# A hybrid decoder layer: gate 21 behind the last pair, values by both token halves, a third early group

## The chip, the cores and the metric

The kernel runs on one core of a Trainium2 chip. The metric is the device time of one execution in microseconds (us). A core's engines work from queues of their own: TensorE (PE) multiplies matrices, VectorE (DVE) and GpSimd (POOL) do elementwise work, ScalarE (ACT) activations and copies, and SyncE (SP) issues the transfers between HBM and the on-chip memory (SBUF). PE writes into banks of PSUM, from which DVE and ACT read.

## The reference

The layer works on 1024 tokens of 1024 features, float32:

```python
h = h + hybrid_mixer(rms_norm(h), ...)
h = h + sq_relu_mlp(rms_norm(h), w_up, w_down)     # 1024 -> 4096 -> 1024
return rms_norm(h)

def hybrid_mixer(u, w_in, ...):
    z = u @ w_in                                   # 1024 -> 3584 columns
    cb, cc, ch = split(z[..., :1536], 3)           # conv group
    rq, rk, rv, rg = split(z[..., 1536:], 4)       # retention group, 4 heads x 128
    y_conv = group_rms_norm(cb * causal_dwconv3(cc * ch, conv_w), ...)
    o = chunkwise_retention(rotary(rq), rotary(rk), rv)
    y_ret = group_rms_norm(o, ...) * silu(rg)
    return concat([y_conv, y_ret]) @ w_out

def sq_relu_mlp(u, w_up, w_down):
    hdn = relu(u @ w_up)
    return (hdn * hdn) @ w_down
```

## The kernel before

Everything lies feature-major: a tile has 128 features as partitions and 512 tokens (a half, `hs[0]` or `hs[1]`) as columns. Every factor of a product is split into two float32r numbers, a high part (ACT, a cast) and a low part (DVE or POOL, a subtraction), and a product is three matmuls: high by high, high by low, low by high. So each weight piece costs an ACT cast into `wh` and a subtraction into `wl`; up to four pieces of each are held (pool `wp`), over four raw buffers `r` that SP refills (pool `rw`).

PE's program runs in this order.

1. **Values** (loop at L342, with the splits at L277). The inputs `xt` are split into `uh` and `ul`, the value weights `wv` into `vh` and `vl`. The splits go through all eight feature tiles k of token half 0, then through all of half 1; so do the 192 matmuls at L349: half 0 into four banks of pool `pm`, half 1 into four of pool `pr`. Squares of x are summed on POOL (`add_square`, L261). After k = 3 of half 1 come the token norms (L359): 16 one-column matmul records that give `ms`, `rtok` and the per-head factors `by_key`, `by_state`, `by_query`.
2. **Queries and keys** (`rot_tiles`, L530): eight tiles of 48 matmuls by `tile_in` (L510), with the retention recurrence (`retention`, L567) woven in.
3. **Turns** (`IN_TURNS`, L40). A number is a whole tile (`whole`, L731: 48 matmuls, four quarters). A pair of numbers is two tiles by seven products in the manner of Strassen (`pair_in`, L811: 7 times 12 matmuls) on sums of inputs held as `U` tiles `t1` to `t4`; its weights are four raw pieces that POOL adds and subtracts in place (`Left`, L197). Tiles 0 to 11 feed the convolution (`conv_h`, `conv_b`) with a group norm (`norm`, L461, two matmuls at L473 and L474), tiles 20 to 23 the gates (`gate`, L708): a product with `R` from PSUM on DVE, a Silu on ACT, a product with the retention output on DVE. Before the pairs, the retention outputs of heads 2 and 3 and the convolution outputs y0 and y1 are spilled to HBM (`put_by`, L854); after the last turn they are fetched back (`get_back`, L863, tiles `back`).
4. **Ends** (`IN_END`): gates 22 and 23, half 0 of both before half 1 of both, in four banks.
5. **Groups** (`group`, L1049): the output projection. Each of four groups makes output tiles j and 4 + j in eight steps of 12 matmuls; the first step of a half needs the splits `yh`, `yl` of that half (`split_y`, L868). Between the steps stands the preparation of the MLP: residual `x2`, sums of squares, tiles `un` and split `U` tiles `11`, `21`, `22`, `t1` to `t4` (`group_todo`, L1027). Groups 0 and 1 finish their `U` tiles there and put `x2` of tiles 4 and 5 aside in HBM (`put_aside`, L1017); for groups 2 and 3 much of it is left to the table `rest` (L1222). Before the groups the PSUM pools `pm` and `pr` (four banks each) are closed with `mixer` (L931) and three pools of 2, 4 and 2 banks opened.
6. **MLP**: first the two early pairs (14 products, with `rest` between them), then blocks that alternate up products (L393) and down products (L1263), and a last block with the final norm.

Where DVE or POOL could do a step, and where in the program a step stands, a planner decides at build time from costs in the class `Engine` (L47): `tick` (L493) starts every waiting task whose inputs should be ready by its own clock `now`, which `slot` advances by 2.72 for each 12 matmuls. The engines then run their queues in that fixed order.

Of the kernel before, what the change touches and what calls it, by code (L numbers as in the profile page):

```python
# [16 lines left out]
P = 128  # L17
D = 1024
# [60 lines left out]
def hybrid_layer(  # L79
# [27 lines left out]
    pm = mixer.enter_context(tc.tile_pool(name="pm", bufs=4, space=PSUM))  # L107
    pr = mixer.enter_context(tc.tile_pool(name="pr", bufs=4, space=PSUM))
# [31 lines left out]
    for k in range(KT):  # L140
# [94 lines left out]
    plan += [next_piece] * (2 * KT)  # L235


    ones = cp.tile([P, 1], F32, name="ones")
    dve.memset(ones, 1.0)
    eps = cp.tile([P, 1], F32, name="eps")  # L240
    dve.memset(eps, EPS)
    act.square(tmp()[:, :1], eps)
# [5 lines left out]
    dve.tensor_copy(blkr, blk)  # L248
    less_g = cp.tile([P, 4], F32, name="less_g")
    dve.tensor_scalar_mul(less_g, sm[:, CG : CG + 4], -1.0)  # L250
    ident = cp.tile([P, P], F32, name="ident")
# [22 lines left out]
    vl = [unit(F32R, "vl") for _ in range(KT // 2)]  # L274
    ssq = xp.tile([P, T], F32, name="ssq")
    R = xp.tile([P, T], F32, name="R")
    for half, sl in enumerate(hs):  # L277
        for k in range(KT):
            vs = hs[k % 2]
            if half == 0 and k == 0:  # L280
                dve.tensor_copy(vh[0][:, vs], wv[0][:, vs])
            split_scaled(xt[k], sm[:, G1 + k : G1 + k + 1], sl, uh[k], ul[k])
            if half == 0:
                if k:
                    act.copy(vh[k // 2][:, vs], wv[k // 2][:, vs])
                dve.tensor_sub(vl[k // 2][:, vs], wv[k // 2][:, vs], f32(vh[k // 2][:, vs]))
            add_square(ssq, xt[k], sl, k == 0)
# [51 lines left out]
    ms = xp.tile([P, NC_], F32, name="ms")  # L339
    r2 = xp.tile([P, NC_], F32, name="r2")  # L340
    by_key, by_state, by_query = (xp.tile([P, NH, NC_], F32, name=s_) for s_ in ("bk", "bz", "bq"))
    for half in range(2):  # L342
        vb = [bank(pr if half else pm) for _ in range(4)]
        for k in range(KT):
            vs = hs[k % 2]
            for a, b in ((uh, vh), (uh, vl), (ul, vh)):
                for i in range(4):
                    tsl = slice((half * 4 + i) * P, (half * 4 + i + 1) * P)
                    nc.tensor.matmul(  # L349
                        vb[i],  # L350
                        a[k][:, tsl],
                        b[k // 2][:, vs],
                        start=(k == 0 and a is uh and b is vh),
                        stop=(k == KT - 1 and a is ul),
                    )
            if half == 1 and k == 3:
                b = bank(pm)
                for c in range(NC_):
                    nc.tensor.matmul(  # L359
                        b[:, c : c + 1], ssq[:, c * P : (c + 1) * P], ones, start=True, stop=True  # L360
                    )
                act.activation(ms, b[:, :NC_], AF.Identity, bias=eps, scale=1.0 / D)
                dve.reciprocal(r2, ms)
                act.activation(rtok, r2, AF.Sqrt)
                for h in range(NH):
                    for i, (to, src) in enumerate(((by_key, r2), (by_state, r2), (by_query, ms))):
                        dve.tensor_scalar_mul(to[:, h, :], src, perhead[:, i, h : h + 1])
        for i in range(4):
            c = half * 4 + i
            act.copy(v[c // 2][:, hs[c % 2]], vb[i])  # L370
    prepare(2)

    R2 = ssq
# [136 lines left out]
    def tile_in(evac):  # L510

        out = [bank() for _ in hs]
        for quarter in range(4):
            c, at = quarter // 2, quarter % 2
            if at == 0:
                piece = parts.pop(0)
            mm(
                piece, out,
                lambda n, k: (uh[4 * c + k][:, hs[n]], ul[4 * c + k][:, hs[n]]),
                quarter == 0, quarter == 3, range(2 * at, 2 * at + 2),  # L520
            )
# [410 lines left out]
    pm = ctx.enter_context(tc.tile_pool(name="pu", bufs=2, space=PSUM))  # L932
    pr = ctx.enter_context(tc.tile_pool(name="pd", bufs=4, space=PSUM))
    pn = ctx.enter_context(tc.tile_pool(name="pn", bufs=2, space=PSUM))
    ct = ctx.enter_context(tc.tile_pool(name="ct", bufs=11))
    kept = ctx.enter_context(tc.tile_pool(name="kept", bufs=5, space=bass.MemoryType.DRAM))
    rv = ctx.enter_context(tc.tile_pool(name="rv", bufs=8))
    temps.append(ct)

# [72 lines left out]
    def source(name, j):  # L1012
        return un[j][:, hi_ if name == "t3" else lo_]
# [13 lines left out]
    def group_todo(j):  # L1027

        hi_of = lambda *names: [lambda x=x: put_hi(x, j, source(x, j)) for x in names]
        lo_of = lambda *names: [lambda x=x: put_lo(x, j, source(x, j)) for x in names]  # L1030
        todo = {
            2: [lambda: put_scaled_hi("11", j, j, 0)],
            3: [lambda: put_scaled_lo("11", j, j, 0)],
            4: [lambda: put_scaled_hi("21", j, 4 + j, 0)],
            5: [lambda: put_scaled_lo("21", j, 4 + j, 0)],
            8: [lambda: sum1(j)] + hi_of("t1"),
            9: lo_of("t1") + [lambda: sum3(j)],
            10: [lambda: sum2(j)],
        }
# [178 lines left out]
    def lo22(j):  # L1218
        put_scaled_lo("22", j, 4 + j, 1)

    rest = [
        todo[32] + lo("t2", dve, 2) + hi("t3", 2),  # L1222
        todo[33] + call(lo22, 2) + todo[34] + call(hi22, 3) + hi("t2", 3),
        call(sum4, 2) + lo("t2", dve, 3) + hi("t3", 3) + lo("t3", dve, 2),
        call(sum4, 3) + call(lo22, 3) + hi("t4", 2, 3) + call(fetch_back, 0, 1),
        lo("t3", dve, 3) + call(fetch_back, 2, 4, 5),
        lo("t4", dve, 2),
        lo("t4", dve, 3),
        call(new_basis, 7),
        call(new_basis, 5),  # L1230
        call(new_basis, 3),
        [],
        [],
        [lambda: v_split(early, 1, 0)],
        [lambda: v_split(early, 1, 1)],
    ]
    for at, (n, p) in enumerate((n, p) for n in MLP_ORDER for p in range(EARLY)):
        b = early[p].product(n)
# [274 lines left out]
```

## Time and profile before

| | |
|---|---|
| runs | 1089.0, 1090.49, 1091.01 us; median 1090.49 |
| the profiled execution's own time | 1089.24 us |
| its span | 1087.5 us |
| PE busy | 1056.8 us, 97% |
| DVE, ACT, POOL busy | 873.3, 469.8, 532.2 us |
| bytes moved | 80.70 MB, 74 GB/s mean |

A row of the timeline gives the start, the duration, engine, line, operation, output and inputs, shape, how many follow each other, and in brackets how long the engine had stood idle before and what ended that. Most rows have L73, the helper that records operations of DVE, ACT and POOL, so tiles tell them apart. A matmul's duration includes its tail; the pace of PE is the distance between starts. The clock of PE (PEclk) is a share of full speed.

### The profile page before, as it was taken

To read this page: it belongs to the slowest core of one execution; us is meant where nothing else is said; L and a number is where in the kernel's file an instruction comes from. 1 tells how busy PE (TensorE), PEld (TensorE's weight loads), DVE (VectorE), ACT (ScalarE), POOL (GpSimd) and SP (SyncE) were. 2 spreads that over 40 slices of the span, in tenths; PEclk is the share of its full clock that TensorE was granted. 3 is DMA by queue.
4 is the path that set the end of the run, shared out by engine and by line. 5 is a ranking of instruction groups with operands and counts; after the bars stand their busy time and mean duration, and the time that the engine had idled before them with its cause. 6 is when DMAs were issued, how large, how long until landed. Compare 5 with 4: busy or idle time off the path is not lost.

```text
span 1087.5 us, 13994 instructions
## 1 busy us (share of the span) xinstructions
PE 1056.8 (97%) x4916; PEld 881.0 (81%) x4916; DVE 873.3 (80%) x1256; ACT 469.8 (43%) x920; POOL 532.2 (49%) x368
## 2 busy tenths in 40 slices
PE   7999999999998799989999999999999999999996
PEld 6888888887887688878888888888888888888886
DVE  7436546798997556599999989989899899899945
ACT  8211445763446444444433343434343434334453
POOL 5234223255652223458538358267276295384543
PEclk9999999999999899999999999999999999999998
DMA  7111122212122625040121211202201301210204
GB/s 271 61 58 39 40 78 69 93 63 78 65 79 100 212 89 183 1 174 20 49 88 39 69 49 49 78 30 59 88 25 49 93 22 48 87 30 13 75 1 156
DMA packets 40022, 80.70 MB, mean 74 GB/s; under 512 B 4496, under 2 KB 6672, under 8 KB 39952
## 3 DMA queue, kind: packets, MB, share of 16 engines
q1 hardware_dynamic: 39952, 79.80, 22.6%
q8 instruction: 39, 0.64, 0.2%
q14 instruction: 31, 0.25, 0.1%
HBM read 70.87 MB, written 8.91 MB: 73 GB/s over the span
## 4 chain that ended last, share of the span: by engine, by line
PE 85%; DVE 6%; issue 4%; ACT 2%; DMA 2%; POOL 1%; SPq 0%; POOLq 0%; DVEq 0%; ACTq 0%
PE b L393 55%; PE b L1263 24%; PE b L349 2%; DVE wl L73 1%; DMA back<-sp 1%; DVE q L73 1%; DVE t L73 1%; PE b L330 1%; DMA xt<-xT 0%; PE b L613 0%; PE b L583 0%; ACT h L73 0%; PE b L651 0%; DVE z L73 0%; PE b L615 0%
## 5 line engine op out<-in xcount | busy, mean ns | idle before, releaser
L73 ACT CAST wh<-r 128x512 fp32r<-128x512 f32 x286 | 176.3, 621 | 336.0 <-PE b L393 141.2
L393 PE MATMUL b<-U,wh 128*128 128x512 f32 x1024 | 315.8, 389 | 3.0 <-DVE U L73 3.0
L73 DVE TENSOR_TENSOR wl<-r,wh 128x512 fp32r<-128x512 f32 x247 | 225.4, 915 | 97.1 <-ACT wh L73 96.4
L73 POOL TENSOR_TENSOR r<-r,r 128x512 f32<-128x512 f32 x136 | 208.7, 1537 | 120.9 <-DVE wl L73 69.9
L1263 PE MATMUL b<-V,wh 128*128 128x512 f32 x784 | 241.8, 389 | 0.4 <-POOL V L73 0.4
L393 PEld LDWEIGHTS b<-U,wh 128*128 128x128 f32 x1024 | 192.0, 188 | 43.2 <-DVE U L73 3.4
L73 DVE TENSOR_TENSOR x<-x,b 128x512 f32<-128x512 f32 (+1 forms) x320 | 198.0, 665 | 27.6 <-PE b L393 24.7
L393 PE MATMUL b<-U,wl 128*128 128x512 f32 x512 | 199.3, 389 | 0.0
L1263 PEld LDWEIGHTS b<-V,wh 128*128 128x128 f32 x784 | 147.1, 188 | 31.8 <-POOL V L73 0.8
L73 POOL TENSOR_TENSOR t<-t,t 128x512 f32<-128x512 f32 x70 | 105.6, 1513 | 102.3 <-ACT t L73 56.3
L1263 PE MATMUL b<-V,wl 128*128 128x512 f32 x392 | 152.5, 389 | 0.0
L73 POOL TENSOR_TENSOR wl<-r,wh 128x512 fp32r<-128x512 f32 x39 | 56.2, 1446 | 160.9 <-ACT wh L73 154.4
L393 PEld LDWEIGHTS b<-U,wl 128*128 128x128 f32 x512 | 96.1, 188 | 20.5 <-POOL wl L73 0.4
L393 PE MATMUL b<-uh,wh 128*128 128x512 f32 x304 | 102.1, 396 | 0.0
L393 PE MATMUL b<-uh,wl 128*128 128x512 f32 x304 | 100.3, 390 | 1.7 <-DVE wl L73 1.7
L393 PE MATMUL b<-ul,wh 128*128 128x512 f32 x304 | 100.4, 390 | 0.0
L1263 PEld LDWEIGHTS b<-V,wl 128*128 128x128 f32 x392 | 73.6, 188 | 15.2
L73 POOL TENSOR_TENSOR V<-t,V 128x512 fp32r<-128x512 f32 x35 | 49.7, 1421 | 67.2 <-ACT V L73 67.1
L73 DVE TENSOR_TENSOR t<-t,b 128x512 f32<-128x512 f32 x112 | 76.0, 678 | 1.7 <-POOL t L73 1.2
L73 ACT ACTIVATE t<-t 128x512 f32<-128x512 f32 x64 | 40.2, 631 | 73.3 <-DVE t L73 72.6
L73 DVE TENSOR_TENSOR V<-t,V 128x512 fp32r<-128x512 f32 x63 | 69.3, 1100 | 0.0
L393 PEld LDWEIGHTS b<-uh,wl 128*128 128x128 f32 x304 | 57.1, 188 | 14.2 <-DVE wl L73 2.1
(163 smaller groups left out, 1422.0 us busy)
## 6 DMA issues: line engine op xcount, KB each, us to landing
r<-w_up_t SPq DMA_DIRECT2D x64, 256.0 KB, 2.6
r<-w_down_t SPq DMA_DIRECT2D x56, 256.0 KB, 2.6
r<-w_in_t SPq DMA_DIRECT2D x48, 256.0 KB, 2.7
xt<-xT SPq DMA_DIRECT2D x16, 256.0 KB, 5.4
xs<-xT SPq DMA_DIRECT2D x8, 512.0 KB, 4.8
r<-w_out_t SPq DMA_DIRECT2D x16, 256.0 KB, 2.6
x<-xT SPq DMA_DIRECT2D x8, 512.0 KB, 7.3
outT<-out SPq DMA_DIRECT2D x6, 512.0 KB, 2.8
```

Of the source, the lines that this page charges most:

```text
L73: return f(out, *args, **kw)
L330: nc.tensor.matmul(b[:, c * P : (c + 1) * P], d, ident, start=True, stop=True)
L349: nc.tensor.matmul(vb[i], a[k][:, tsl], b[k // 2][:, vs], start=(k == 0 and a is uh and b is vh), stop=(k == KT - 1 and a is ul),)
L393: nc.tensor.matmul(b, a[:, k, :], rhs(n, k)[r], start=(start and i == 0), stop=(stop and i == len(ops) - 1),)
L1263: nc.tensor.matmul(b, a, r, start=(i == 0), stop=(i == len(ops) - 1))
```

## The change

Five edits are made together.

- **Turns.** Gate 21 goes behind the last pair, so all four pairs follow each other and gates 21, 22, 23 are the last three tiles. The spilled tiles are asked for right after the last pair, before gate 21.
- **Values.** Loads, splits and matmuls go k by k with both halves of a k together, in eight banks at once. The token norms move into the first query tile, after its second quarter.
- **Zeros first.** Ten 128 x 128 float32 matmuls of a tile of zeros are PE's first work.
- **Kept banks.** `pm` and `pr` stay open through the groups; the three new PSUM pools are opened between the groups and the MLP.
- **Third early group.** Group 2 finishes its `U` tiles as groups 0 and 1 do, and `x2` of tile 6 is put aside as well (one more store and load of 512 KB). `rest` becomes shorter, and the first split of the hidden values stands two products earlier.

```diff
-IN_TURNS = [0, 1, 2, 3, 20, (4, 5), (6, 7), 21, (8, 9), (10, 11)]
+IN_TURNS = [0, 1, 2, 3, 20, (4, 5), (6, 7), (8, 9), (10, 11), 21]
+WARM = 10
...
-    for k in range(KT):
         nc.sync.dma_start(xt[k][:, hs[1]], xT[k * P : (k + 1) * P, hs[1]])
...
+    blk = tmp()[:, :P]
+    dve.memset(blk, 0.0)
+    b = bank(pr)
+    for _ in range(WARM):
+        nc.tensor.matmul(b[:, :P], blk, blk, start=True, stop=True)
...
-    for half, sl in enumerate(hs):
-        for k in range(KT):
+    for k in range(KT):
+        for half, sl in enumerate(hs):
...
-    for half in range(2):
-        vb = [bank(pr if half else pm) for _ in range(4)]
-        for k in range(KT):
-            vs = hs[k % 2]
+    vb = [bank(pr if i >= 4 else pm) for i in range(NC_)]
+    for k in range(KT):
+        vs = hs[k % 2]
+        for half in range(2):
...
+            if quarter == 1 and once:
+                once.pop()()
...
-    for turn in IN_TURNS:
+    for at, turn in enumerate(IN_TURNS):
...
-    for h in (2, 3):
-        force(("by", ("o", h)))
-        o_n[h, 0] = o_n[h, 1] = get_back(("o", h))
-    for i in range(2):
-        force(("by", ("y", i)))
-        y[i] = get_back(("y", i))
-        got["back", i] = now[0] + 5.0
+        if at == len(IN_TURNS) - 2:
+            for h in (2, 3):
+                force(("by", ("o", h)))
+                o_n[h, 0] = o_n[h, 1] = get_back(("o", h))
+            for i in range(2):
+                force(("by", ("y", i)))
+                y[i] = get_back(("y", i))
+                got["back", i] = now[0] + 10.0
...
-        if j < 2:
+        if j < 3:
...
-    todo[30] = [lambda: put_hi("t2", 2, source("t2", 2)), lambda: put_scaled_hi("22", 2, 6, 1)]
     for j in range(4):
         group(j)
+    banks_.close()
+    pm = ctx.enter_context(tc.tile_pool(name="pu", bufs=2, space=PSUM))
+    pr = ctx.enter_context(tc.tile_pool(name="pd", bufs=4, space=PSUM))
+    pn = ctx.enter_context(tc.tile_pool(name="pn", bufs=2, space=PSUM))
```

What the edits do to the queues is shown at three places. First DVE at the start of the program: `blkr` is a constant of the group norms, `vh` and `vl` are the parts of the value weights, `ul` the low parts of the inputs. Before:

```order
L73 MEMSET ones 128x1
L73 MEMSET eps 128x1
L73 MEMSET t_131 128x128
L73 MEMSET t_131 64x64 x2
L73 CAST blkr<-t_131 128x128
L73 TENSOR_SCALAR less_g<-sm 128x4
L73 CAST vh_160<-wv_90 128x512
L73 SCALAR_TENSOR_TENSOR ul_152<-xt_82,sm,uh_144 128x512
L73 TENSOR_TENSOR vl_164<-wv_90,vh_160 128x512
L73 SCALAR_TENSOR_TENSOR ul_153<-xt_83,sm,uh_145 128x512
L73 TENSOR_TENSOR vl_164<-wv_90,vh_160 128x512
```

And in the changed kernel:

```order
L74 MEMSET t_125 128x128
L74 MEMSET t_138 128x128
L74 MEMSET t_138 64x64 x2
L74 CAST blkr<-t_138 128x128
L74 MEMSET ones 128x1
L74 MEMSET eps 128x1
L74 TENSOR_SCALAR less_g<-sm 128x4
L74 CAST vh_173<-wv_90 128x512
L74 SCALAR_TENSOR_TENSOR ul_165<-xt_82,sm,uh_157 128x512
L74 TENSOR_TENSOR vl_177<-wv_90,vh_173 128x512
L74 SCALAR_TENSOR_TENSOR ul_165<-xt_82,sm,uh_157 128x512
L74 SCALAR_TENSOR_TENSOR ul_166<-xt_83,sm,uh_158 128x512
```

The zeros (`t_125`) are DVE's first operation, and each k now has two `ul` (one for each half) beside one `vl`.

Second, SP around the return of the spilled tiles: `r` are weight pieces (the last `w_in` pieces are those of gates 22 and 23), `back` the tiles that come back. Before:

```order
L159 DMA r_2810<-w_in_t 128x512
L159 DMA r_2834<-w_in_t 128x512
L159 DMA r_2861<-w_out_t 128x512
L159 DMA r_2882<-w_out_t 128x512
L159 DMA r_2907<-w_out_t 128x512
L159 DMA r_2929<-w_out_t 128x512
L865 DMA back_2943<-sp_1978 128x1024
L865 DMA back_2945<-sp_1980 128x1024
L865 DMA back_2947<-sp_2208 128x1024
L865 DMA back_2949<-sp_2524 128x1024
```

And in the changed kernel:

```order
L160 DMA r_2805<-w_in_t 128x512
L160 DMA r_2826<-w_in_t 128x512
L160 DMA r_2851<-w_out_t 128x512
L160 DMA r_2873<-w_out_t 128x512
L875 DMA back_2887<-sp_1991 128x1024
L875 DMA back_2889<-sp_1993 128x1024
L875 DMA back_2891<-sp_2221 128x1024
L875 DMA back_2893<-sp_2584 128x1024
L160 DMA r_2929<-w_out_t 128x512
L160 DMA r_2959<-w_out_t 128x512
```

The four fetches stand two weight pieces, so one whole tile of 48 matmuls, earlier in the program.

Third, DVE between the last evacuation of the groups (the output sum into the last `x` tile) and the low part of the `t2` tile of group 3 (`U_3923` before, `U_3943` now), which the third kind of early product needs. Before:

```order
L73 TENSOR_TENSOR x_3156<-x_3156,b_3794 128x512
L73 TENSOR_TENSOR wl_3885<-r_3404,wh_3884 128x512
L73 TENSOR_TENSOR un_3753<-un_3753 128x512
L73 TENSOR_TENSOR U_3836<-un_3581,U_3836 128x512
L73 TENSOR_TENSOR wl_3912<-r_3588,wh_3911 128x512
L73 TENSOR_TENSOR U_3891<-un_3753,U_3891 128x512
L73 SCALAR_TENSOR_TENSOR un_3753<-x_3156,sm,un_3753 128x512
L73 SCALAR_TENSOR_TENSOR U_3838<-x_3155,sm,U_3838 128x512
L73 SCALAR_TENSOR_TENSOR un_3753<-x_3156,sm,un_3753 128x512
L73 TENSOR_TENSOR wl_3941<-r_3408,wh_3940 128x512
L73 SCALAR_TENSOR_TENSOR un_3581<-x_3155,sm,un_3581 128x512
L73 TENSOR_TENSOR U_3923<-un_3753,U_3923 128x512
```

And in the changed kernel:

```order
L74 TENSOR_TENSOR x_3169<-x_3169,b_3804 128x512
L74 TENSOR_TENSOR wl_3909<-r_3406,wh_3908 128x512
L74 TENSOR_TENSOR un_3755<-un_3755 128x512
L74 TENSOR_TENSOR wl_3935<-r_3590,wh_3934 128x512
L74 TENSOR_TENSOR U_3915<-un_3755,U_3915 128x512
L74 SCALAR_TENSOR_TENSOR un_3755<-x_3169,sm,un_3755 128x512 x2
L74 TENSOR_TENSOR wl_3961<-r_3410,wh_3960 128x512
L74 TENSOR_TENSOR U_3943<-un_3755,U_3943 128x512
```

The three steps of group 2 (`U_3836`, `U_3838` and `un_3581`) are gone from between: 11 operations follow the evacuation before, eight now.

More of the change, by code (lines that the diff above doesn't have):

```diff
@@ L106, in hybrid_layer @@
     mixer = ctx.enter_context(ExitStack())
-    pm = mixer.enter_context(tc.tile_pool(name="pm", bufs=4, space=PSUM))
-    pr = mixer.enter_context(tc.tile_pool(name="pr", bufs=4, space=PSUM))
+    banks_ = ctx.enter_context(ExitStack())
+    pm = banks_.enter_context(tc.tile_pool(name="pm", bufs=4, space=PSUM))
+    pr = banks_.enter_context(tc.tile_pool(name="pr", bufs=4, space=PSUM))
     tp = mixer.enter_context(tc.tile_pool(name="tp", bufs=6))
@@ L235, in hybrid_layer @@
     plan += [next_piece] * (2 * KT)
[L238 to L242, printed above, removed]
+    blk = tmp()[:, :P]
[3 more added lines that the diff above has]
+        nc.tensor.matmul(b[:, :P], blk, blk, start=True, stop=True)
     blk = tmp()[:, :P]
@@ L248, in hybrid_layer @@
     dve.tensor_copy(blkr, blk)
+    ones = cp.tile([P, 1], F32, name="ones")
+    dve.memset(ones, 1.0)
+    eps = cp.tile([P, 1], F32, name="eps")
+    dve.memset(eps, EPS)
+    act.square(tmp()[:, :1], eps)
     less_g = cp.tile([P, 4], F32, name="less_g")
@@ L341, in hybrid_layer @@
     by_key, by_state, by_query = (xp.tile([P, NH, NC_], F32, name=s_) for s_ in ("bk", "bz", "bq"))
-    for half in range(2):
-        vb = [bank(pr if half else pm) for _ in range(4)]
-        for k in range(KT):
-            vs = hs[k % 2]
+    vb = [bank(pr if i >= 4 else pm) for i in range(NC_)]
+    for k in range(KT):
+        vs = hs[k % 2]
+        for half in range(2):
             for a, b in ((uh, vh), (uh, vl), (ul, vh)):
-                for i in range(4):
-                    tsl = slice((half * 4 + i) * P, (half * 4 + i + 1) * P)
+                for i in range(half * 4, half * 4 + 4):
                     nc.tensor.matmul(
                         vb[i],
-                        a[k][:, tsl],
+                        a[k][:, i * P : (i + 1) * P],
                         b[k // 2][:, vs],
@@ L355, in hybrid_layer, with token_norms @@
                     )
[L356 to L370, printed above, removed]
+    for c in range(NC_):
+        act.copy(v[c // 2][:, hs[c % 2]], vb[c])
+    def token_norms():
+        b = bank(pr)
+        for c in range(NC_):
+            nc.tensor.matmul(
+                b[:, c : c + 1], ssq[:, c * P : (c + 1) * P], ones, start=True, stop=True
+            )
+        act.activation(ms, b[:, :NC_], AF.Identity, bias=eps, scale=1.0 / D)
+        dve.reciprocal(r2, ms)
+        act.activation(rtok, r2, AF.Sqrt)
+        for h in range(NH):
+            for i, (to, src) in enumerate(((by_key, r2), (by_state, r2), (by_query, ms))):
+                dve.tensor_scalar_mul(to[:, h, :], src, perhead[:, i, h : h + 1])
+    once = [token_norms]
     prepare(2)
@@ L931, in hybrid_layer @@
     mixer.close()
-    pm = ctx.enter_context(tc.tile_pool(name="pu", bufs=2, space=PSUM))
-    pr = ctx.enter_context(tc.tile_pool(name="pd", bufs=4, space=PSUM))
-    pn = ctx.enter_context(tc.tile_pool(name="pn", bufs=2, space=PSUM))
     ct = ctx.enter_context(tc.tile_pool(name="ct", bufs=11))
-    kept = ctx.enter_context(tc.tile_pool(name="kept", bufs=5, space=bass.MemoryType.DRAM))
+    kept = ctx.enter_context(tc.tile_pool(name="kept", bufs=6, space=bass.MemoryType.DRAM))
     rv = ctx.enter_context(tc.tile_pool(name="rv", bufs=8))
@@ L1221, in hybrid_layer @@
     rest = [
[L1222 to L1228, printed above, removed]
+        todo[32] + call(hi22, 3),
+        todo[33] + todo[34] + hi("t2", 3),
+        lo("t2", dve, 3) + hi("t3", 3) + call(lo22, 3),
+        call(sum4, 3) + lo("t3", dve, 3) + hi("t4", 3) + call(fetch_back, 0, 1),
+        lo("t4", dve, 3) + call(fetch_back, 2, 4, 5, 6),
+        [],
+        [],
         call(new_basis, 7),
@@ L1231, in hybrid_layer @@
         call(new_basis, 3),
-        [],
-        [],
-        [lambda: v_split(early, 1, 0)],
-        [lambda: v_split(early, 1, 1)],
+        [lambda: v_split(early, 1, 0)],
+        [lambda: v_split(early, 1, 1)],
+        [],
+        [],
     ]
```

## The prediction

> **What bounds the kernel now.** I read the page's first rows, then the list of PE's waits, then PE's busy time by windows, and last the timeline around each wait.
>
> ```profile
> span 1087.5 us, 13994 instructions
> PE 1056.8 (97%) x4916; PEld 881.0 (81%) x4916; DVE 873.3 (80%) x1256; ACT 469.8 (43%) x920; POOL 532.2 (49%) x368
> ```
>
> PE is busy 97% of the span, so only PE's idle time, its slow stretches or its own number of matmuls can give anything. The list of PE's waits (line and operand, what released it, total, times, longest):
>
> ```profile
> PE b L393 <- DVE z L73: 9.1, 1, 9.1
> PE b L349 <- DVE vh L73: 6.2, 1, 6.2
> PE b L393 <- DVE U L73: 3.0, 1, 3.0
> PE b L393 <- DVE wl L73: 1.7, 1, 1.7
> ```
>
> Three single waits carry most of the idle time: the first group's start, the first value product, the early MLP. By windows (busy us and records of PE, granted clock, DMA share, GB/s) the program's start, the stop before the groups and the MLP read:
>
> ```profile
> 0.00:20.00 20.00, 13.77 (x51) 1.00 0.88 315
> 340.00:360.00 20.00, 10.87 (x47) 0.80 0.15 44
> 520.00:800.00 280.00, 280.00 (x1237) 231.67 (x1236) 260.29 (x366) 110.68 (x192) 154.41 (x104) 1.00 0.19 58
> ```
>
> The last row has all engines (PE, PEld, DVE, ACT, POOL): in the MLP's steady state PE never stops and DVE is busy 260.29 of 280. No edit takes a matmul out of it, so I book nothing there. PE's pace is 0.2267 us for each 512-column matmul, from 12 that take 2.72 in the chain:
>
> ```profile
> 495.77 2.72 PE b L1263 x12
> ```
>
> All sums below are against the profiled execution's 1089.24 us. The median of the runs is 1.25 above it, which is added at the end. About 0.2%, 2.2 us, is what a measurement of this kernel can tell from no change.
>
> **Zeros first and values by both halves: -2.3.** DVE's first operation, PE's timeline at the start, and the price of small float32 matmuls:
>
> ```profile
> 0.81 0.06 DVE L73 MEMSET ones<- 128x1 f32 x1 [0.81 <-PEq L1501]
> 6.24 2.05 PE L349 MATMUL b<-vh,uh 128*128 128x512 f32 x4 [6.24 <-DVE vh L73]
> 8.08 1.91 PE L349 MATMUL b<-vl,uh 128*128 128x512 f32 x4
> 9.78 1.59 PE L349 MATMUL b<-vh,ul 128*128 128x512 f32 x4
> 11.21 1.09 PE L349 MATMUL b<-vh,uh 128*128 128x512 f32 x4
> 106.00 0.60 PE L583 MATMUL b<-q,q 128*128 128x128 f32 x4
> 106.44 0.38 PE L588 MATMUL b<-ident,q 128*128 128x128 f32 x2
> ```
>
> The first twelve matmuls take 11.21 - 6.24 = 4.97 us, the same number at pace 2.72: 2.25 us are lost to a slow start. The zeros are float32 128 x 128 matmuls, as at L583: two of them (four records) take 106.44 - 106.00 = 0.44, so 0.22 each at full speed, 0.44 at half. Ten at half speed are 4.4 us. DVE's first operation runs at 0.8, so the zeros run from about 1.2 to 5.6, ahead of the first value matmul at 6.24, whose operand (the cast of the first value weights, released by its load) does not come earlier. If the start is slow only because PE has been idle, the zeros take the slow stretch and the value matmuls begin at pace: 2.25 gained.
>
> The order by k changes what DVE owes: two `ul` and one `vl` for each k.
>
> ```profile
> 6.67 0.69 DVE L73 TENSOR_TENSOR vl<-wv,vh 128x512 fp32r<-128x512 f32 x1
> 26.92 1.78 DVE L73 TENSOR_TENSOR vl<-wv,vh 128x512 fp32r<-128x512 f32 x1
> ```
>
> At 1.78 for the slow ones three are 5.3, against 24 matmuls of 0.2267 = 5.44: PE stays covered, barely. A short wait may come at the first `vl`, which PE reaches sooner. The token norms' matmuls only change place. Bounds 0 to 2.6; I take 2.3, since the loss is read directly.
>
> The Trainium skill ("TensorE: Matmul & The Clock Gate", section on the HAM clock gate) says that PE has full clock only after a busy window of about 3.4 us, and that the window is free-running, so that the number of slow matmuls varies from run to run. The two rows of slow starts here (4.97 us, and 3.4 us at 359.23 below) agree with some such stretch; by that rule 4.4 us of zeros may or may not hold one whole window, so by the page the gain is an estimate between 0 and 2.25. I book the row's 2.25 and keep the other as a rival.
>
> **Gate 21 behind the pairs, kept banks: -10.9.** PE's stop before the groups, SP's fetch, the chain of waits, and two operations of the engines between:
>
> ```profile
> 349.71 0.39 PE L393 MATMUL b<-uh,wl 128*128 128x512 f32 x1
> 359.23 0.77 PE L393 MATMUL b<-yh,wh 128*128 128x512 f32 x1 [9.13 <-DVE z L73]
> 362.63 0.40 PE L393 MATMUL b<-yh,wl 128*128 128x512 f32 x1
> 331.53 1.86 SPq L865 DMA_DIRECT2D back<-sp  x4
> 332.95 7.47 DMA back<-sp
> 358.41 0.68 DVE L73 TENSOR_TENSOR z<-b,R 128x512 f32<-128x512 f32 x1
> ```
>
> The last gate's matmul starts at 349.71; at pace the next would start at 349.94, and it starts at 359.23: 9.29. Its eight first steps to 362.63 take 3.40 instead of 1.81: 1.59 more from the slow restart (granted clock 0.80 in that window). Together 10.9.
>
> What was late is a chain: the fetches are issued at 331.53, 18 us before PE ends; the last data land 7.5 us after that; then ACT and DVE do splits and gate products of the fetched tiles in turn, and the last product from PSUM (358.41) frees the bank that the group needs. The change issues the fetches one whole tile of 48 matmuls earlier: 48 x 0.2267 = 10.9 us of PE. Were the chain as long as now (from the landing at 332.95 + 7.47 = 340.42 to 358.41 + 0.68 = 359.09, 18.7 us), it would end at 359.1 - 10.9 = 348.2, which is 1.7 us ahead of PE's 349.9. And it gets shorter at its end: with kept banks, the groups' first banks are those that the last gates' half 0 left, not those of a pool that must first be closed, so the products of half 1 no longer stand in front of the first step of a group; the splits of half 1 are needed 48 matmuls, 10.9 us, after those of half 0. So the wait has a reason to go whole, and with it the slow restart. What could take its place are the residual's loads, which wait for the last gate product. If two or three operations (0.7 to 1.8 us each) still come late, up to 3 stay: bounds 8 to 10.9. I take the upper end, because the margin is positive even with the chain at its present length.
>
> **Third early group: -2.5.** PE's second wait, with the DVE operations that leave from in front of its operand, and ACT's:
>
> ```profile
> 462.66 0.40 PE L393 MATMUL b<-U,wh 128*128 128x512 f32 x1
> 466.02 0.50 PE L393 MATMUL b<-U,wh 128*128 128x512 f32 x1 [2.96 <-DVE U L73]
> 458.57 0.68 DVE L73 TENSOR_TENSOR U<-un,U 128x512 fp32r<-128x512 f32 x1
> 459.84 0.74 DVE L73 SCALAR_TENSOR_TENSOR U<-x,sm,U 128x512 fp32r<-128x512 f32 x1
> 463.54 0.75 DVE L73 SCALAR_TENSOR_TENSOR un<-x,sm,un 128x512 f32<-128x512 f32 x1
> 448.28 0.60 ACT L73 CAST U<-un 128x512 fp32r<-128x512 f32 x1
> 448.79 0.72 ACT L73 ACTIVATE U<-x,sm 128x512 fp32r<-128x512 f32 x1
> 450.90 0.68 DVE L73 TENSOR_TENSOR x<-x,b 128x512 f32<-128x512 f32 x1
> ```
>
> The stop is 466.02 - 462.66 - 0.23 = 3.13. Three DVE operations go, 0.68 + 0.74 + 0.75 = 2.2, and two ACT ones of 1.3 ahead of a weight cast on which DVE waits, of which about 1.1 shows. That is 3.3 against 3.13. New there: the three PSUM pools open now between groups and MLP, so the second early product waits for the last evacuation (450.90 + 0.68 = 451.58, while PE was there at 450.61): 0 to 1.0 of wait. I take 0.6 for it, so 2.5, with bounds 1 to 3.1. The same three steps of group 2 now lie inside the groups, where DVE has room (its share is 80% over the span); the extra 512 KB store and load meet DMA engines that are 15% to 19% busy in the windows above.
>
> The hidden values' first split stands two products earlier, and the wait for it (0.4 in the list of waits) goes: -0.4.
>
> ```profile
> PE b L1263 <- POOL V L73: 0.4, 1, 0.4
> ```
>
> **Four pairs in a row: +1.5.** Between the second and third pair gate 21 gave DVE and POOL air, 48 matmuls with few operations. The two last pairs by windows (PE, PEld, DVE, ACT, POOL), and DVE operations alone and beside POOL:
>
> ```profile
> 288.30:307.80 19.50, 19.50 (x88) 16.15 (x87) 17.11 (x19) 10.29 (x16) 12.19 (x9) 1.00 0.17 54
> 307.80:327.40 19.60, 19.60 (x88) 16.25 (x87) 17.72 (x23) 7.92 (x15) 8.95 (x7) 1.00 0.28 81
> 282.23 1.78 DVE L73 TENSOR_TENSOR wl<-r,wh 128x512 fp32r<-128x512 f32 x1
> 280.02 3.43 POOL L73 TENSOR_TENSOR r<-r,r 128x512 f32<-128x512 f32 x2
> 293.27 1.28 DVE L73 TENSOR_TENSOR z<-b,R 128x512 f32<-128x512 f32 x2
> 294.65 1.41 DVE L73 SCALAR_TENSOR_TENSOR q<-z,sm,q 128x512 f32<-128x512 f32 x2
> ```
>
> DVE has 19.50 - 17.11 = 2.4 us free in one and 1.9 in the other. By the new order it makes four more `wl` in the third pair (POOL made them): 2.7 to 7.1 us, at 0.68 or at 1.78 each, the latter where POOL works at the same time, as at 282.23; gate 21's two pairs of operations, 1.28 + 1.41 = 2.7, leave. So the pair exceeds PE by between -2.4 and 2.0. Followed operation by operation, one norm's split is ready about 1.2 us after PE wants it, and the fourth pair has 0 to 1 more. Bounds 0 to 6 (the latter if DVE also meets POOL in four other places, 4 x 1.1 on top of 1.5); I take 1.5.
>
> **Sum.** 1089.24 - 2.3 - 10.9 - 2.5 - 0.4 + 1.5 = 1074.6; with 1.25, 1075.9. By the ends: all gains high and no loss gives 1089.24 - 2.6 - 10.9 - 3.1 - 0.4 + 1.25 = 1073.5; one term near its bad end gives 1077 to 1081.
>
> **Rivals.**
>
> *Zeros don't help.* If the slow start stays, 2.25 comes back: 1078.2. For it: the granted clock shows 1.00 in the first window, so the slow start is not seen in that column. Against: the pace of the first twelve (0.41 mean) is that of the slow restart at 359.23, where the column shows 0.80. Chance 0.12.
>
> *DVE late in the pairs.* Two to four more operations at the slow price in each pair, 2.2 x 2 to 2.2 x 4 beside the 2.0 of the bound above: 6.4 to 10.8 in place of 1.5, so 1080.8 to 1085.2. For it: DVE is 88% to 90% busy there already. Chance 0.14.
>
> *Half of the boundary stays.* The fetch is early, but the norm of tile 11 and the gates' activations still stand in one chain on ACT ; half of 10.9, some 5 us, stays: 1080.9. Chance 0.06.
>
> *It doesn't do what it says.* The fetches wait on SP behind something late and the boundary stays whole: 1075.9 + 10.9 = 1086.8, and with no gain at the start 1089. Chance 0.04.
>
> *Slower.* DVE becomes the bound of the pairs. Without the pairs' term the change gains 16.1. It is slower once pairs three and four lose more than that, about 8 us each; beyond the 2.0 above, at 1.1 for each operation that runs at 1.78 instead of 0.68, that is more than six slow operations in each of both pairs, and eight for a loss of over 2.2 us. Nine give 2.0 + 2 x 9.9 = 21.8: 1089.24 - 16.1 + 21.8 + 1.25 = 1096.2. For it: a pair has 19 to 23 DVE operations, and POOL is busy 9 to 12 of 19.5. Against: at that share of POOL most were fast or hidden before. Chance 0.07.
>
> **The numbers.** The forecast, 1075.9, has 0.57; its own range is 1073.5 to 1081. The range given, 1072.5 (one us of run spread below the best sum) to 1084.5, takes in the zeros' rival, the half boundary and most of the late pairs, and leaves out about 0.17. Faster by over 0.2% (below 1088.3): 0.57 + 0.12 + 0.14 + 0.06 + 0.01 = 0.90; within 0.2%: 0.03; slower: 0.07.
>
> **What would show it.** Right: no wait of PE on `z` at the first group; value matmuls 0.91 us apart by fours from the first on; the wait on `U` under 1 us; PE busy in full in both last pairs but for one wait of about 1 us on `s`. Wrong: a new line of over 2 us in the list of waits in the last two pairs (DVE `wl`, `s`) or at the groups' start (DVE `yl`, `back`), or a restart at half pace after any of them.

## The result, and the profile of the changed kernel

The changed kernel takes 1079.91 us (median; 1079.54 to 1082.14), the kernel before in the same comparison 1090.22. The ratio is 0.9912, with a 95% interval of 0.9899 to 0.9925: 10.3 us less, clear of the 0.2% that can be told from no change. The forecast was 1075.9 in a range of 1072.5 to 1084.5. The sign and the range held; of the 14.6 us of gain that it foresaw, 4.3 did not come.

The profiled execution of the changed kernel is the longest of its four (1082.14). The same kernel ran again among the experiments, with a profile of 1080.29; what differs between the two is told below. First two rows of the page of the first profile, and of its list of PE's waits those that bear on the change (total us, times, longest):

```profile
span 1080.3 us, 14040 instructions
PE 1060.6 (98%) x4936; PEld 882.7 (82%) x4936; DVE 881.2 (82%) x1255; ACT 463.3 (43%) x916; POOL 540.3 (50%) x370
PE b L401 <- DVE z L74: 2.3, 1, 2.3
PE b L401 <- DVE x L74: 1.2, 2, 0.7
PE b L355 <- DVE vh L74: 1.1, 1, 1.1
PE b L401 <- DVE wl L74: 1.1, 1, 1.1
PE b L481 <- ACT s L74: 1.0, 1, 1.0
```

The three large waits of before are gone (9.1 at the first group, 6.2 at the first value product, 3.0 on `U`); the second is filled by the zeros and not shortened, since the first value product starts no earlier. The wait on `z` that heads the list has the old one's name but another place. The stretches of PE's timeline, from start to start (the groups to the end of their last matmul), say where the time went:

| stretch of PE, us | before | changed, first profile | changed, second |
|---|---|---|---|
| start to first value product | 6.24 | 6.28 | 5.96 |
| to the first product of the first pair | 234.41 | 232.00 | 232.08 |
| to the first product of the groups | 118.58 | 115.30 | 113.78 |
| the groups | 88.83 | 87.20 | 87.20 |
| to the MLP's first down product | 47.55 | 45.98 | 45.96 |
| to the first product of the last block | 531.56 | 533.68 | 533.65 |

**The start.** PE's timeline in the first profile:

```profile
1.05 4.09 PE L244 MATMUL b<-t 128*128 128x128 f32 x20 [1.05 <-DVE t L74]
6.28 1.15 PE L355 MATMUL b<-vh,uh 128*128 128x512 f32 x4 [1.13 <-DVE vh L74]
9.39 0.84 PE L355 MATMUL b<-vh,uh 128*128 128x512 f32 x3
```

The zeros take 4.09 us, from 1.05, nearly at the half pace that was assumed; the first twelve value matmuls take 9.39 - 6.28 = 3.11 us in place of 4.97.

**The groups' start.** Their first matmul follows the last gate's at pace, 0.23 us after it:

```profile
353.35 0.39 PE L401 MATMUL b<-uh,wl 128*128 128x512 f32 x1
353.58 0.39 PE L401 MATMUL b<-yh,wh 128*128 128x512 f32 x1
```

**Where a new stop stands.** At gate 21, one matmul after the last pair. PE's rows, and those of DVE and ACT before it:

```profile
315.94 0.39 PE L401 MATMUL b<-uh,wh 128*128 128x512 f32 x1
318.60 0.80 PE L401 MATMUL b<-uh,wh 128*128 128x512 f32 x1 [2.27 <-DVE z L74]
310.57 2.45 DVE L74 SCALAR_TENSOR_TENSOR cv<-z,sm,cv 128x511 f32<-128x511 f32 x2 [0.79 <-ACT cv L74]
312.95 0.68 DVE L74 SCALAR_TENSOR_TENSOR r<-b,r 128x512 f32<-128x512 f32 x1
316.36 2.18 DVE L74 TENSOR_TENSOR z<-z,b 128x512 f32<-128x512 f32 x3
309.82 0.72 ACT L74 ACTIVATE cv<-z,sm 128x512 f32<-128x512 f32 x1 [6.26 <-DVE z L74]
310.96 0.68 ACT L74 ACTIVATE r<-b,eps 128x512 f32<-128x512 f32 x1
```

Gate 21's second bank is one that the fourth pair's third product held (the program takes pm's four banks in turn); DVE frees it with the third of the three `z<-z,b` from 316.36. These stand in DVE's queue behind a norm (`r<-b,r` and two more), and that behind two taps of the convolution (`cv<-z,sm,cv`). The taps need ACT's `cv`, for which ACT had waited 6.26 us until DVE was done with `z`; the norm needs ACT's `r`, which stands behind that `cv`. In the second profile the wait is the same, but not what follows. PE by windows (busy, records, granted clock, DMA share, GB/s), of the first:

```profile
318.00:320.00 2.00, 1.40 (x3) 0.61 0.00 0
320.00:322.00 2.00, 2.00 (x6) 0.54 0.00 0
```

and of the second:

```profile
318.00:320.00 2.00, 1.68 (x7) 1.00 0.00 0
320.00:322.00 2.00, 2.00 (x10) 1.00 0.00 0
```

After 2.27 us of waiting PE restarts at half clock in one execution, after 2.29 us at full clock in the other; that is the 1.5 us between the two columns of the table in the third stretch.

### The profile page after: what moved, and what is told of

Read it like the earlier page. It is cut to its first block, busy times and chain, and to the rows that moved or that the text cites. A ratio compares the mean times of both kernels' runs of the same rounds, so it can differ in the third digit from the quotient of the medians.

```text
span 1080.3 us, 14040 instructions
## 1 busy us (share of the span) xinstructions
PE 1060.6 (98%) x4936; PEld 882.7 (82%) x4936; DVE 881.2 (82%) x1255; ACT 463.3 (43%) x916; POOL 540.3 (50%) x370
## 4 chain that ended last, share of the span: by engine, by line
PE 80%; DVE 11%; issue 3%; POOL 3%; ACT 2%; DMA 1%; POOLq 0%; DVEq 0%; SPq 0%; ACTq 0%
PE b L401 50%; PE b L1274 23%; PE b L355 4%; DVE z L74 2%; DVE wl L74 2%; POOL r L74 1%; POOL z L74 1%; DVE t L74 1%; DVE x L74 1%; DVE xs L74 1%; DVE U L74 1%; DVE q L74 1%; ACT h L74 1%; PE b L337 1%; DVE m L74 1%
## 5 line engine op out<-in xcount | busy, mean ns | idle before, releaser
L74 DVE TENSOR_TENSOR wl<-r,wh 128x512 fp32r<-128x512 f32 x251 | 233.3, 932 | 90.9 <-ACT wh L74 90.0
L74 POOL TENSOR_TENSOR wl<-r,wh 128x512 fp32r<-128x512 f32 x35 | 49.1, 1408 | 159.2 <-ACT wh L74 151.9
```

The source lines that it names most:

```text
L74: return f(out, *args, **kw)
```

## The experiments

All times are medians; "before" is the kernel before on the same chip, and each ratio has its 95% interval. The changed kernel's 1080.02 us is of the first chip (1090.97 before); on the other three chips the kernel before took 1090.65, 1091.0 and 1088.86, so across chips a difference of 1 us to the changed kernel says little. The stretches are those of the table.

**The changed kernel again** (no edit).

> The changed kernel again, as the yardstick for the runs beside it: 1079.5 to 1081 us by the first measurement. The theory says that its runs differ by whether PE restarts slowly after the 2.3 us wait at gate 21's first matmul (1.4 us); the rival is that its profiled execution, 2.2 us above its median, was late in other places.

1080.02 us, 0.9906 (0.9889 to 0.9923). As the theory said: of the 1.85 us between the two profiled executions, 1.52 lie in the stretch with the restart at gate 21.

**Without the zeros.**

```diff
-WARM = 10
+WARM = 0
```

> The changed kernel without the ten zero matmuls. Theory: the slow start of the value matmuls returns, 4.97 us for the first twelve in place of 3.1, and the time is 1.9 to 2.3 us above the changed kernel's. Rival: the new order of the values already hides the start (DVE's splits are what PE waits for there), so the time stays within 0.7 us.

1083.20 us, 0.9936 (0.9920 to 0.9952), 3.2 above the changed kernel beside it, more than the theory's 1.9 to 2.3. The first twelve matmuls take 9.93 - 5.30 = 4.63 us again:

```profile
5.30 2.05 PE L355 MATMUL b<-vh,uh 128*128 128x512 f32 x4 [5.30 <-DVE vh L74]
9.93 1.07 PE L355 MATMUL b<-vh,uh 128*128 128x512 f32 x4
```

So the zeros do what they are for, and the new order of the values alone doesn't. From the first value product to the first pair it is 233.55 us: 1.5 more than in the changed kernel's second profile, and 0.9 less than before. The rest of the 3.2 stands elsewhere: this execution also restarted slowly at gate 21, and the third stretch is 115.66 for 113.78. The one run of the six with a mean granted clock of 0.997 took 1081.50, 1.8 above the changed kernel's fastest, 1079.70, which has the same clock; the other five have 0.995 or 0.996. So the zeros are worth some 1.5 to 1.8 us.

**The old pools closed before the groups, as before the change.** The three pools are opened after `mixer.close()` again.

> The changed kernel with the PSUM pools closed before the groups, as before the change. Theory: the early fetch carries most of the 10.9 us at the groups' start, the kept banks only the evacuations of the last gates; PE waits 2 to 4 us at the first group (with or without a slow restart), the two waits of 0.5 and 0.7 us at the first early products go, and the time is 1 to 4 us above the changed kernel's. Rival: the kept banks carry most of it, and 6 us or more come back.

1085.01 us, 0.9953 (0.9938 to 0.9969): 5.0 above the changed kernel, between theory (1 to 4) and rival (6). The wait is in the range, but a slow restart adds 1.48 us (the groups take 88.68 for 87.20), and there is a wait of 1.1 on `U`. The last gate product, on DVE, is again what PE waits for:

```profile
354.38 0.76 PE L401 MATMUL b<-yh,wh 128*128 128x512 f32 x1 [2.58 <-DVE z L74]
353.56 0.68 DVE L74 TENSOR_TENSOR z<-b,R 128x512 f32<-128x512 f32 x1
459.19 0.50 PE L401 MATMUL b<-U,wh 128*128 128x512 f32 x1 [1.13 <-DVE U L74]
```

**The kept banks alone, in the kernel before.** `pm` and `pr` leave `mixer`, and the three new pools open after the groups; nothing else changes.

> The kernel before with one edit alone: the old PSUM pools stay open through the groups. Theory, after the runs with the turns back and with the late fetch: the 9.1 us at the first group were a wait for banks that the closing of the pools imposed, not for the fetched tiles; the wait falls to 2.4 to 3.5 us without a long restart, and the time is 6.5 to 8 us below before: 1082.5 to 1084. Rival, the prediction's chain: without an earlier fetch the splits are late as well, most of the wait stays, and the time is above 1087.

1082.22 us, 0.9928 (0.9915 to 0.9940): 8.8 us below before by the medians and 7.9 by the ratio, by this one edit; the theory had 6.5 to 8. What is left at the first group is a wait for weights, first ACT's cast and then POOL's low part:

```profile
351.64 0.55 PE L394 MATMUL b<-yh,wh 128*128 128x512 f32 x1 [2.05 <-ACT wh L73]
353.19 0.79 PE L394 MATMUL b<-yh,wl 128*128 128x512 f32 x1 [0.57 <-POOL wl L73]
358.19 0.68 DVE L73 TENSOR_TENSOR z<-b,R 128x512 f32<-128x512 f32 x1
```

DVE's last gate product still comes as late as in the kernel before (358.19 here, 358.41 there), since the fetch is as late; PE no longer waits for it. This is the plainest evidence against the prediction's chain of fetched tiles as the cause of the 9.1 us. One part of the theory, "without a long restart", was a miss: PE runs at half clock (granted 0.50) from 352 to 358 us, and the groups take 91.04 us, 3.8 more than in the changed kernel.

**The fetch late, all else as changed.** The block of fetches goes behind the loop over the turns again.

> The changed kernel with the four fetches after the last turn again, behind gate 21, all else as changed. Theory: fetch and kept banks each carry a part of the 10.9 us at the groups' start; with the fetch 10.9 us later the splits of the fetched tiles and the last gates' products come late, and PE waits 3 to 8 us at the first group, so 3 to 9 us above the changed kernel's 1080. Rival: the kept banks alone do it, and the time stays within 1 us.

1081.13 us, 0.9916 (0.9903 to 0.9929): the theory, 3 to 9 us, is refuted. The rival's 1 us is passed by 0.1, which the intervals don't tell apart, and the profiled execution restarted at half clock at gate 21. SP issues the fetches 7.0 us later than in the changed kernel (331.55 in place of 324.52), and there is no wait at the first group in this profile. SP's rows, of the changed kernel's second profile and of this one:

```profile
324.52 1.85 SPq L875 DMA_DIRECT2D back<-sp  x4
```

```profile
331.55 1.95 SPq L875 DMA_DIRECT2D back<-sp  x4
```

**The turns and the fetch as before, the other four edits kept.**

```diff
-IN_TURNS = [0, 1, 2, 3, 20, (4, 5), (6, 7), (8, 9), (10, 11), 21]
+IN_TURNS = [0, 1, 2, 3, 20, (4, 5), (6, 7), 21, (8, 9), (10, 11)]
```

> The changed kernel with the order of turns and the place of the fetches as before the change (gate 21 between the second and third pair, fetches after the last pair), the other four edits kept. Theory: the 4.9 us that the four pairs in a row lose (waits of 1.0, 0.2, 0.3 and 2.3 us and their restarts) go, and 5 to 9 us come back at the groups' start: 1080 to 1085. Rival: gate 21's place has no price in the pairs (what is late there is late for another reason), and the time is 1085 to 1091.

1080.24 us, 0.9903 (0.9887 to 0.9919), the changed kernel's time: this edit, the largest in the diff, nets nothing. Both halves of the theory show. The third and fourth pair have none of the waits on `s` and `z`, and at the first group PE waits 2.40 and 0.81 and restarts slowly:

```profile
349.39 0.50 PE L401 MATMUL b<-yh,wh 128*128 128x512 f32 x1 [2.40 <-ACT wh L74]
350.93 0.50 PE L401 MATMUL b<-yh,wl 128*128 128x512 f32 x1 [0.81 <-POOL wl L74]
```

From the first pair to the groups' end it is 111.32 + 90.03 = 201.35 us, in the changed kernel 113.78 + 87.20 = 200.98.

**Less work for DVE in the last pairs.** Two of three taps are left out for channel tiles 2 and 3, as the expectation says; the order of the rest is the same.

> The changed kernel without two of the three taps of the convolution for channel tiles 2 and 3 (eight DVE operations left out around the third and fourth pair, some 9 us of DVE time; the order of all others is the same). Theory: DVE's queue is what PE waits for in the last two pairs and at gate 21; the waits of 1.0 and 2.3 us on s and z fall below 0.3, and the time is 1075 to 1077. Rival: PE waits there for ACT or for a chain through the norm, and the time stays within 1 us of 1080.

1078.79 us, 0.9897 (0.9884 to 0.9911): 1.2 less, neither theory nor rival. The waits of 1.0, 0.2 and 0.3 us around the norms go, so those were DVE's load. The wait on `z` stays, at 2.31, though DVE is now idle ahead of the norm:

```profile
309.74 0.69 DVE L74 SCALAR_TENSOR_TENSOR r<-b,r 128x512 f32<-128x512 f32 x1 [2.55 <-ACT r L74]
316.00 0.50 PE L401 MATMUL b<-uh,wh 128*128 128x512 f32 x1 [2.31 <-DVE z L74]
```

So it isn't the taps that hold the bank: without them the chain through ACT's queue takes as long. That chain starts when DVE is done with `z` at 307.19, after a stretch without a pause, so DVE's load ahead of it may still count; it wasn't tried apart.

**Gate 21's second bank from the other pool.**

```diff
-        tile_in(evac)
+        tile_in(evac, (None, pr) if f == 21 else (None, None))
```

> The changed kernel with one bank moved: the second output bank of gate 21 is taken from the pool pr instead of pm, so that it isn't the bank that held the fourth pair's third product until DVE added it. Theory, after the run without taps: PE's wait of 2.3 us on z at gate 21 is for that one bank, whose release stands in DVE's queue behind the norm of tile 8, which waits for ACT; so the wait and the slow restart after it go, and the time is 2.3 to 3.9 us below the changed kernel's 1080.0: 1076 to 1077.8. Rival: DVE's lateness only shows at the next use of a bank, and the time stays within 1 us.

1079.94 us, 0.9903 (0.9888 to 0.9919): no gain. The mechanism is as described, since the wait is gone (PE runs through gate 21 without a stop), but the time isn't: a tile later PE waits for the norm of tile 11, and restarts at half clock. Its rows and windows:

```profile
327.15 0.50 PE L481 MATMUL b<-s,blkr 128*128 128x512 f32 x1 [0.90 <-ACT s L74]
327.88 0.50 PE L482 MATMUL b<-s,blkr 128*128 128x512 f32 x1 [0.22 <-DVE s L74]
329.21 0.80 PE L482 MATMUL b<-s,blkr 128*128 128x512 f32 x1 [0.23 <-DVE s L74]
325.00:330.00 5.00, 3.55 (x11) 0.91 0.95 323
330.00:335.00 5.00, 5.00 (x18) 0.74 0.64 243
```

**Only two groups finished early.** `j < 3` is `j < 2` again, with the old table `rest` (and so with the first split at its old place).

> The changed kernel with only groups 0 and 1 finished early, as before the change. Theory: what the third group saves at the early products (3.1 us of wait) is given back at once, half of it at the banks, half in the first 70 us of the MLP, where DVE, at 93% of the time, is behind PE by 2 us; so this kernel is within 0.7 us of the changed one, though it shows the wait of about 3 us on U again. Rival, the prediction's term: 2.5 us slower.

1080.06 us, 0.9906 (0.9889 to 0.9923), against 1080.02: as the theory said. The wait on `U` is there, 1.75 us, and the stretches show the exchange: 47.53 to the first down product (45.96 with three groups), then 531.70 to the last block (533.65).

```profile
456.83 0.50 PE L401 MATMUL b<-U,wh 128*128 128x512 f32 x1 [1.75 <-DVE U L74]
```

**The new pools in another order.** The kernel that ran opens them in the order pn, pd, pu. The order that the expectation names, pu, pn, pd, was not run.

> The changed kernel with its three new PSUM pools opened in the order pu, pn, pd, by which the first two early products no longer need the banks of the last evacuations. Theory: the two waits on x (0.5 and 0.7 us) go, but DVE is behind PE at the start of the MLP, so most of it is given back within 70 us: 1079.4 to 1080.3. Rival: the waits are plain loss, and the time is 1.2 to 1.6 us lower, 1078.6.

1083.76 us, 0.9941 (0.9928 to 0.9954): 3.7 slower, which neither had; but since the order is another one, this settles neither. The two waits became one, for the last evacuation of all:

```profile
443.90 0.70 PE L401 MATMUL b<-U,wh 128*128 128x512 f32 x2 [4.10 <-DVE x L74]
443.08 0.68 DVE L74 TENSOR_TENSOR x<-x,b 128x512 f32<-128x512 f32 x1
```

The first early product takes its bank from pu. With pu opened last, it waits for the bank that is freed last; that the order of opening decides which bank this is, is argued from the row and not tested further. Of the 4.3 us more up to the first down product (50.29), 1.7 came back by the last block (531.97 for 533.65).

**No pool closed at all** (`pn = pm`).

> The changed kernel with the two old PSUM pools kept to the end (pn is pm, nothing is closed or opened after the groups), so that no early product needs a bank that has just been evacuated. Theory: the two waits on x (0.5 and 0.7 us) go without a new one, but in the MLP's first blocks DVE is the slower engine, so more than half is given back there: 1079 to 1080. Rival: plain loss, 1078.3 to 1078.9.

1080.02 us, 0.9906 (0.9891 to 0.9920). The two waits on `x` go, but a wait of 1.12 on `U` stands behind them, and the 45.76 us to the first down product are hardly less than 45.96: the theory's time, by an earlier exchange than it named.

```profile
456.75 0.50 PE L401 MATMUL b<-U,wh 128*128 128x512 f32 x1 [1.12 <-DVE U L74]
```

**A better version: kept banks, the old order of turns, and the fetch before the last pair.** `IN_TURNS` as in the run with the turns back, the fetches where the changed kernel's loop puts them (behind the last turn but one).

> The changed kernel with gate 21 back between the second and third pair, and the four fetches a whole pair earlier than before the change: between the third and the fourth pair. Theory: with kept banks and this order of turns, what PE waits for at the first group (2.4 us for ACT's weight cast, 0.8 us for POOL's low part, and a slow restart of 1.7 us) is ACT's queue, in which the splits of the fetched tiles stand; with the fetch ahead of the last pair they leave it, nothing is lost in the pairs, and the time is 1075.3 to 1077.5, below both kernels. Rival: the norm of the last pair and the last gates fill ACT's queue by themselves, or the splits disturb the last pair, and the time stays at 1080 or above.

1076.47 us, 0.9880 (0.9858 to 0.9902): clear of before, and by the medians 3.5 us below the changed kernel's 1080.02. By the ratios (0.9880 for 0.9906) it is 2.8 us, and the two intervals overlap a little, but all four runs (1075.63 to 1077.23) lie below all eight runs of the changed kernel. The profile shows more plainly where it comes from. From the first pair to the groups' end it is 108.53 + 88.30 = 196.83 us, 4.2 less than in the changed kernel. SP fetches at 309.73, and PE's waits at the groups' start are 0.35 and 0.15:

```profile
309.73 1.81 SPq L875 DMA_DIRECT2D back<-sp  x4
347.74 0.50 PE L401 MATMUL b<-yh,wl 128*128 128x512 f32 x1 [0.35 <-POOL wl L74]
350.00 0.50 PE L401 MATMUL b<-yl,wh 128*128 128x512 f32 x1 [0.15 <-DVE yl L74]
```

## Why the prediction was right, and where it failed

**The start** (-2.3 forecast): right in size, and in cause for the larger part. 234.41 becomes 232.00 and 232.08, so 2.3 to 2.4 us. By the stretch of the run without zeros (233.55), the zeros carry 1.5 of it and the other edits 0.9, most likely the new order of the values, which the sum put at nothing. The value matmuls do not begin at pace: the first twelve take 3.11 us, not 2.72. So the 2.25 booked for the zeros was too much, and that the sum fits is in part luck.

**The groups' start** (-10.9): right in size, wrong in cause. The whole stop goes. But the step "What was late is a chain: the fetches" fails: with the fetch 7 us later PE doesn't wait there, and with the kept banks alone 8.8 us are gained. The closing of two pools made the first group wait for banks, the last of which came free when the late chain ended. The prediction named this as a help at the chain's end; it was the main thing. Its working for the chain alone, done 1.7 us ahead of PE, is refuted by the run with the pools closed as before: there the last gate product ends at 354.24, while PE could have gone on at 351.64, so 2.6 us behind. One reason is that the fetch comes 7.0 us earlier by SP's rows, not 10.9. (The working's "7.5 us after that" for the landing is a slip: from 331.53 to 340.42 it is 8.9; its sum uses 340.42.) That the size came out although the cause was wrong is luck: the edit that did it stood in the same term. The rest of the stop goes by the new order of turns, or else by a fetch a whole pair earlier, as in the better version: with neither, 2.0 to 2.4 us of waiting for ACT's cast and 0.6 to 0.8 for POOL's low part stay there, with a slow restart.

**Four pairs in a row** (+1.5): the term that was mis-sized most. Of the two stretches from the first pair to the groups' end, before has 207.41 and the changed kernel 200.98 (second profile). That is 6.4 less, where the stop of 10.9 and 0.8 at an earlier `wl` (1.68, now 0.92) went: the pairs cost 5.2, in the first profile 6.6. The wait on `s`, about 1.2 us foreseen, came as 1.0 and 0.2. What the working left out is the bank at gate 21: "the fourth pair has 0 to 1 more" looked at DVE's time and not at whose bank the next tile takes. The wait is 2.3 us, with 1.5 more where the clock falls; it is the sign of being wrong that the prediction named, a new wait of over 2 us, one matmul behind the last pair. That this eats the whole gain of the edit at the groups' start is shown by the run with the turns back.

**Third early group and first split** (-2.5 and -0.4): failed. The operations that leave were booked at 3.3 us, the whole wait on `U`. Where the pools are closed as before, so that no bank wait stands ahead of it, that wait falls from 2.96 to 1.13; with no pool closed it is 1.12. So they are worth 1.8. In the changed kernel the rest is hidden by the two bank waits (0.47 and 0.70, 0.6 foreseen in all), and PE is at the first down product 1.6 us earlier, in place of 2.9. The 0.4 of the first split was read from the wrong place: the one wait of the list for POOL's `V` stands at 995.30 in the kernel before, far behind the early products, and it is still there:

```profile
995.30 0.50 PE L1263 MATMUL b<-V,wh 128*128 128x512 f32 x1 [0.42 <-POOL V L73]
986.77 0.50 PE L1274 MATMUL b<-V,wh 128*128 128x512 f32 x1 [0.40 <-POOL V L74]
```

Then 2.1 us are given back: "I book nothing there" was the error. DVE is busy 93% of the time from 520 to 800 us, and nearly without a pause from 490 to 510, soon after the first down product, so it can't catch up where PE arrives earlier. The second profile shows DVE's busy time in these 20 us (the two rows of windows), PE waiting where it didn't before, and the evacuation on DVE, with work right ahead of it, that ends just before PE goes on. The evacuation on ACT that the last wait names had itself waited for DVE:

```profile
490.00:500.00 10.00, 9.96 (x13) 1.00 0.03 10
500.00:510.00 10.00, 10.00 (x14) 1.00 0.22 69
504.62 0.70 PE L401 MATMUL b<-U,wh 128*128 128x512 f32 x2 [0.45 <-DVE t L74]
502.10 1.78 DVE L74 TENSOR_TENSOR V<-t,V 128x512 fp32r<-128x512 f32 x1
503.80 0.67 DVE L74 TENSOR_TENSOR t<-t,b 128x512 f32<-128x512 f32 x1
522.44 0.70 PE L401 MATMUL b<-U,wh 128*128 128x512 f32 x2 [0.73 <-ACT t L74]
521.73 0.63 ACT L74 ACTIVATE t<-t 128x512 f32<-128x512 f32 x1 [4.19 <-DVE t L74]
```

The run with two groups is the check: it reaches the first down product 1.6 us later and has 2.0 us less from there to the last block.

The sum of the table's rows by the second profile: -0.3 - 2.3 - 4.8 - 1.6 - 1.6 + 2.1 = -8.5 on PE, and the spans, 1087.5 and 1078.5, are 9.0 apart. Of the rivals, none came as written. The nearest is the late pairs, with fewer slow operations and a bank in their place.

What stays open: how much of the pairs' loss an order of ACT's queue with the norm's `r` ahead of `cv` would save, and what the pools in the order pu, pn, pd would do; neither was tried.

## What to carry to other kernels

A wait that a trace puts down to an evacuation may be for the bank and not for the data: ask what forces that bank (here the closing of a pool, and the turn of four banks), and change that alone first. One edit of a few lines gave 8.8 us alone, of 10.3 for all five, by the medians. A wait taken from an engine's path returns where the next engine is nearly full: beside a DVE that is 93% busy, the time saved ahead of a stage was given back within it. And an edit with two effects should be measured apart: the new order of turns gave some 5 us at one place and took some 5 at another.

## What the runs showed of the hardware

Nine profiled executions have the wait of 2.3 us at gate 21. After it PE ran at half clock for about 3 us in six of them and at full clock in three, with waits of 2.27 to 2.32 us throughout. The kernel before ran on at full clock after 2.96 us, three waits of 0.9, 0.2 and 0.2 us within 3 us were enough for half clock in the run with the moved bank, and waits of 2.05 and 0.57 us in the run with the kept banks alone were followed by over 6 us of it. So the length of a wait alone doesn't decide. The Trainium skill ("TensorE: Matmul & The Clock Gate", the part on the HAM clock gate) has PE fall back after at least one idle window of about 3.4 us; it also calls the window free-running. The second agrees with a wait that is followed now by the one and now by the other; the first doesn't, since waits of 2.3 us sufficed. A slow restart at gate 21 adds about 1.5 us, which may be part of why the runs of the changed kernel lie up to 2.6 us apart.
